# Up's first half ahead for 20 pairs instead of 8, modulation columns asked for by running estimates, and high priority for the latency chains

## The chip, the cores and the metric

The kernel runs on one core of a Trainium2 chip. The metric is the device time in microseconds, median of three runs; below it stands beside the span of one profiled execution of the same program. The engines are TensorE (PE for its matmuls, PEld for its weight loads), VectorE (DVE), ScalarE (ACT), GpSimd (POOL, hardly used) and SyncE (SP), whose queue issues every large transfer.

## The reference, cut to what matters

One decoder layer on 256 tokens of width 2048, in float32:

```
mod = silu(c) @ w_ada + b_ada                    # 6 x 2048: shift, scale, gate, twice
h = rmsnorm(x) * (1 + sc1) + sh1
q_sb,k_sb,v_sb, q_ds,k_ds,v_ds, q_ix,k_ix,w_ix = split(h @ w_in)
o_sb = stick_breaking_attention(q_sb, k_sb, v_sb)   # 8 heads of 128; log-sigmoid, suffix sums, exp
score = sum_h w_ix * relu(rope(q_ix) @ rope(k_ix).T)    # 16 index heads of 64
o_ds = attention(rope(q_ds), rope(k_ds), v_ds) over the 64 best scores of each token   # 8 heads
x = x + g1 * (concat[rmsnorm(o_sb), rmsnorm(o_ds)] @ w_out)
h2 = rmsnorm(x) * (1 + sc2) + sh2
u = h2 @ w_up                                    # 2 x 5504 columns: gate and value
u = conv_b + causal depthwise conv of width 3 over u
x = x + g2 * ((silu(gate) * val) @ w_down)
return rmsnorm(x)
```

## The kernel before, in words

**Weights.** Every weight is read once, in pieces of 128x2048 float32 (1 MB), each by one DMA that SP issues (`load`, L135) into one of four `raw` buffers. A float32 product is made of three products of a narrower type: `split` (L142) takes 1024 columns of a piece, ACT casts them to the high part (L145), DVE subtracts to get the low part (L146), and PE runs high x high, high x low and low x high. In `nat` (L149) the activations are stationary and 512 weight columns move; in `trn` (L171) the weights are stationary and 256 tokens move, in three matmuls; in `fold` (L157) high and low of the tokens stand side by side, so that one matmul of 512 columns and one of 256 do the same.

**Modulation.** The 96 columns of `mod` (128 values each) are independent of all else. One column is either a 1 MB load with one multiply-and-accumulate on DVE (`ada`, L223, tile `wa`), or it belongs to a group of four columns done on PE (`ada_pe`, L194, tiles `wg`, `ap`, `rw`, `aq`): four 1 MB loads with 4 matmuls each, a copy by ACT, four transposes and a short reduction. The list `PEG` names the groups on PE by their first column. Columns wait in two queues (`pending`, `pend_pe`); `pump` (L378), called at fixed places of the program, sends out as many of each as two strings of digits (`PLAN`) say for that call, and `need` sends out what is required at once.

**Order of the work.** A tile scheduler turns the program into one instruction list per engine; a list is executed in order. `order` adds a dependence where one is wanted. The stages, with the stretch that each has in the profile: norm, first half (8 of 16 k tiles) of the projections A, B, V, QK (0 to 168 us); A and B for the second half (to 222); index scores, top-64 and the sparse (DSA) attention, a long chain over DVE, ACT and PE, with the second half of V as other work for PE (to 284); second half of QK, one head per step, and the eight stick-breaking heads `sb_head` (L666, tiles z, u, o) (to 381); the first halves of the output projection O, on the DSA heads; the norm of the stick-breaking heads, `rms_b` with the tiles `rsb` and then `norm_o` (tiles os, osh, osl) (to 404); the rest of O and the first residual (to 475); the second norm and h2 (to 484); Up, 43 pairs of gate and value tiles U with the convolution and silu (to 968); Down, W (to 1207); the last norm.

**Up before.** A pair takes two 1 MB loads, `wU` f,0 (k tiles 0 to 7) and f,1 (k tiles 8 to 15). For the first `G0` = 8 pairs the first halves run ahead into eight PSUM banks, with `trn`; h2 for k = 8 to 15 is made meanwhile, as its modulation columns come; then the second halves follow into the same banks. The other 35 pairs run both halves together with `fold` in two banks.

Of the kernel before, what the change touches and what calls it, by code (L numbers as in the profile page):

```python
# [19 lines left out]
P = 128  # L20
# [23 lines left out]
PEG = [4, 40, 48, 76, 52]  # L44
# [10 lines left out]
def layer(ctx: ExitStack, tc: tile.TileContext, a, out):  # L55
# [52 lines left out]

    def rms_b(sqs_, width, y, name, tag):
# [82 lines left out]
    def ada_pe(j0, q, st={}):  # L194
# [4 lines left out]
        w = load(a["wg"][PEG.index(j0), q], 2048, f"wg{j0}{q}")  # L199
# [23 lines left out]
    def ada(j):  # L223
        w = load(a["wa"][j], 2048, f"wa{j}")
# [69 lines left out]

    def rope(x, t, H, rd, o, name):
# [49 lines left out]

    def put(half, dst, src, scale=1.0):
# [5 lines left out]
        elif scale == 1.0:  # L352
# [5 lines left out]
    credit = [0.0, 0.0]  # L358
# [17 lines left out]
    step = [0]  # L376

    def pump():  # L378
        i = step[0]
        step[0] += 1  # L380
        for c, l in enumerate((pending, pend_pe)):
            if i < len(PLAN[c]):
                n = int(PLAN[c][i])
            else:
                credit[c] += RATE[c]
                n = int(credit[c])
                credit[c] -= n
            for _ in range(min(n, len(l))):
                emit(l)
# [127 lines left out]

    for t in range(NT):
# [27 lines left out]
    for t in range(NT):  # L546
# [27 lines left out]
        V.tensor_tensor(out=sacc[0], in0=sacc[0], in1=sacc[1], op=ALU.add)  # L574
        cur, nxt = sacc
# [27 lines left out]
    for t in range(NT):  # L603
# [29 lines left out]
        for g in range(2):  # L633
# [16 lines left out]

    def norm_o(o, rb_, oh, ol):
        for h in range(0, NH, 4):
# [115 lines left out]
    def h2_make(k):  # L768
# [8 lines left out]
        modulate(h2[k // 4][:, k % 4, 0, :], h2[k // 4][:, k % 4, 1, :], x1T[i][:, j, :], am, r2p if k < 3 else r2, sh,  # L777
# [17 lines left out]

    G0 = 8
    uacc = {}

    def do_U(f, i):

        if i == 0:
            uacc[f] = [bank(f"U{f}{gv}") for gv in range(2)] if f >= G0 else bank(f"U{f}")
        w = load(a["wU"][f, i], 2048, f"wU{f}{i}")
        steps = []
        for gv in range(2):
# [5 lines left out]
            for j in range(8):  # L811
# [23 lines left out]
    for f in range(FT):  # L835
# [4 lines left out]
        pump()  # L840
# [5 lines left out]
        else:  # L846
            u = acc
# [120 lines left out]
```

## Time and profile before

| | us |
|---|---|
| median of three runs (1219.72 to 1223.4) | 1222.13 |
| the profiled execution, its own time | 1222.48 |
| its span, first to last instruction | 1220.7 |
| PE busy (95%) | 1154.4 |
| DVE busy (72%) | 879.5 |
| ACT busy (52%) | 632.2 |
| read from HBM | 300.24 MB, 248 GB/s over the span |

PE is busy for 95% of the span, so the 66 us in which it is not are to be looked for by stage, and beside them what PE does that could be done elsewhere or in fewer matmuls. Busy shares of the other engines are means over stages of different kinds.

### The profile page before, as it was taken

How to read it: one execution, taken by the hardware profiler on the slowest of the kernel's cores; microseconds unless marked ns; L12 is line 12 of the kernel's file. 1: busy time of each engine (PE TensorE's matmuls, PEld its weight loads, DVE VectorE, ACT ScalarE, POOL GpSimd, SP SyncE). 2: the span in 40 equal slices, each digit the busy share in tenths (PEclk: the TensorE clock that was granted, in tenths of full speed). 3: DMA queues.
4: the chain of work that ended last, by engine and by line, in shares of the span. 5: the costliest groups of instructions: out<-in, count | busy, mean ns of one | idle time of the engine just before them, and what ended most of it. 6: DMA issues, size and time to landing. Idle time of an engine off the chain costs nothing.

```text
span 1220.7 us, 17725 instructions
## 1 busy us (share of the span) xinstructions
PE 1154.4 (95%) x7120; PEld 1018.6 (83%) x7120; DVE 879.5 (72%) x1267; ACT 632.2 (52%) x1004; POOL 0.2 (0%) x4
## 2 busy tenths in 40 slices
PE   3699999899999797999999999999999999999996
PEld 2578997668878797999888888888888888888885
DVE  4877787689766698878789787787876745454543
ACT  3356554457465344456565556555655644444441
POOL 0000000000000000000000000000000000000000
PEclk9799999899999898999999999999999999999998
DMA  8988899668788498776568666675665555555541
GB/s 308 391 318 333 330 324 335 256 222 329 260 341 331 141 346 306 246 275 238 177 246 336 241 210 225 222 254 208 246 224 202 178 198 183 196 184 189 191 139 69
DMA packets 43282, 303.48 MB, mean 249 GB/s; under 512 B 4928, under 2 KB 5440, under 8 KB 7232
## 3 DMA queue, kind: packets, MB, share of 16 engines
q1 hardware_dynamic: 43200, 302.35, 68.1%
q8 instruction: 55, 0.90, 0.3%
q14 instruction: 27, 0.22, 0.0%
HBM read 300.24 MB, written 2.10 MB: 248 GB/s over the span
## 4 chain that ended last, share of the span: by engine, by line
PE 89%; DVE 6%; ACT 3%; DMA 1%; issue 1%; SPq 0%; DVEq 0%; ACTq 0%
PE U L168 21%; PE W L168 13%; PE U L166 11%; PE W L166 7%; PE U L173 3%; PE U L174 3%; PE U L175 3%; PE O L174 3%; PE O L175 3%; PE QK L173 3%; PE QK L175 3%; PE O L173 3%; PE QK L174 3%; DVE wa L225 2%; PE ap L202 1%; PE A L151 1%
## 5 line engine op out<-in xcount | busy, mean ns | idle before, releaser
L225 DVE SCALAR_TENSOR_TENSOR wa<-wa,scb 128x2048 f32<-128x2048 f32 x76 | 173.2, 2284 | 3.8 <-DMA wa<-wa 3.5
L844 ACT COPY u<-U 128x256 f32<-128x256 f32 x70 | 26.1, 372 | 116.6 <-PE U L168 116.6
L845 DVE TENSOR_TENSOR u<-U,u 128x256 f32<-128x256 f32 x70 | 29.3, 420 | 58.7 <-ACT u L844 58.7
L855 DVE SCALAR_TENSOR_TENSOR uc<-u,par,uc 128x255 f32<-128x255 f32 (+1 forms) x140 | 63.8, 478 | 0.8
L851 ACT ACTIVATE uc<-u,par 128x256 f32<-128x256 f32 x70 | 41.9, 601 | 0.0
L862 ACT CAST aT<-uc 128x256 fp32r<-128x256 f32 x43 | 17.4, 404 | 33.3 <-DVE uc L861 33.3
L323 ACT ACTIVATE amul<-mod,b,par 128x1 f32<-128x1 f32 x32 | 12.1, 385 | 42.8 <-DVE wa L225 42.6
L890 DVE SCALAR_TENSOR_TENSOR x1T<-W,mod,x1T 128x256 f32<-128x256 f32 x16 | 7.7, 481 | 31.1 <-PE W L166 31.1
L741 ACT ACTIVATE x2q<-x1T 128x256 f32<-128x256 f32 x15 | 6.3, 418 | 39.1 <-DVE x1T L736 39.0
L326 ACT ACTIVATE mod<-mod,par 128x1 f32<-128x1 f32 x32 | 8.5, 294 | 30.5 <-DVE wa L225 29.4
L202 PE MATMUL ap<-wg,csil 128*32 128x512 f32 x160 | 23.5, 642 | 0.7 <-DMA wg<-wg 0.5
L857 ACT ACTIVATE uc<-uc 128x256 f32<-128x256 f32 x43 | 17.9, 416 | 7.7 <-DVE uc L855 7.6
L861 DVE TENSOR_TENSOR uc<-uc 128x256 f32<-128x256 f32 x43 | 18.2, 422 | 2.8
L863 DVE TENSOR_TENSOR aT<-uc,aT 128x256 fp32r<-128x256 f32 x43 | 18.0, 418 | 0.8 <-ACT aT L862 0.7
L855 DVE SCALAR_TENSOR_TENSOR uc<-U,par,uc 128x255 f32<-128x255 f32 (+1 forms) x32 | 15.0, 478 | 1.0 <-ACT uc L851 0.6
L686 ACT ACTIVATE sbt<-sbt 128x384 f32<-128x384 f32 x8 | 4.2, 525 | 20.6 <-DVE sbt L685 20.6
L202 PEld LDWEIGHTS ap<-wg,csil 128*32 128x32 f32 x160 | 4.3, 115 | 9.4 <-issue 7.0
L736 DVE SCALAR_TENSOR_TENSOR x1T<-O,mod,xT 128x256 f32<-128x256 f32 x16 | 7.0, 479 | 6.7 <-PE O L175 6.7
L555 PE MATMUL rel<-ws,qixT 64*128 64x128 f32 (+1 forms) x64 | 9.8, 390 | 1.5 <-ACT rl L560 1.5
L207 ACT COPY rw<-ap 128x512 f32<-128x512 f32 x5 | 2.9, 581 | 15.5 <-PE ap L202 15.5
L283 PE MATMUL cb<-ident,csil 128*128 128x128 f32 x16 | 3.6, 423 | 7.6 <-DMA ident<-ident 7.6
L151 PE MATMUL A<-wA00h,hh 128*128 128x512 f32 x4 | 2.5, 669 | 8.5 <-ACT hh L318 8.5
(2810 smaller groups left out, 4042.8 us busy)
## 6 DMA issues: line engine op xcount, KB each, us to landing
wU<-wU SPq DMA_DIRECT2D x86, 1024.0 KB, 4.8
wa<-wa SPq DMA_DIRECT2D x76, 1024.0 KB, 6.3
wD<-wD SPq DMA_DIRECT2D x43, 1024.0 KB, 4.8
wg<-wg SPq DMA_DIRECT2D x20, 1024.0 KB, 7.1
wA<-wA SPq DMA_DIRECT2D x16, 1024.0 KB, 6.7
wQK<-wQK SPq DMA_DIRECT2D x16, 1024.0 KB, 6.1
wO<-wO SPq DMA_DIRECT2D x16, 1024.0 KB, 5.7
xT<-xT SPq DMA_DIRECT2D x4, 512.0 KB, 6.0
```

The lines of the kernel that those rows point to most:

```text
L166: T.matmul(pt[:, 1, :], lhsT=wl, rhs=x[:, 0, :], start=False, stop=stop)
L168: T.matmul(pt, lhsT=wh, rhs=x, start=first, stop=stop)
L173: T.matmul(pt, lhsT=wh, rhs=xh, start=first, stop=False)
L174: T.matmul(pt, lhsT=wh, rhs=xl, start=False, stop=False)
L175: T.matmul(pt, lhsT=wl, rhs=xh, start=False, stop=last)
L202: T.matmul(pt[32 * j:32 * j + 32, :], lhsT=csil[:, k:k + 1].to_broadcast([P, 32]), rhs=w[:, j * 512:(j + 1) * 512], start=q == 0, stop=q == 3)
L225: i = V.scalar_tensor_tensor(out=w, in0=w, scalar=1.0, in1=scb, op0=ALU.mult, op1=ALU.mult, accum_out=mod[:, j:j + 1])
L844: A.copy(out=u[:, gv, :], in_=acc[gv][:, 1, :])
L845: V.tensor_tensor(out=u[:, gv, :], in0=acc[gv][:, 0, :], in1=u[:, gv, :], op=ALU.add)
L851: A.activation(uc[:, gv, :], u[:, gv, :], AF.Identity, scale=par[:, PCW + 3 * i + 2:PCW + 3 * i + 3], bias=par[:, PCB + i:PCB + i + 1])
L855: V.scalar_tensor_tensor(out=uc[:, gv, sft:S], in0=u[:, gv, 0:S - sft], scalar=par[:, o:o + 1], in1=uc[:, gv, sft:S], op0=ALU.mult, op1=AL ...
L861: V.tensor_tensor(out=uc[:, 1, :], in0=uc[:, 0, :], in1=uc[:, 1, :], op=ALU.mult)
```

## The change

1. Two PE groups fewer: columns 48 to 51, 76 to 79 and 52 to 55 go to DVE, columns 44 to 47 to PE. So there are 12 `wg` loads instead of 20, and 84 `wa` loads instead of 76, as many megabytes in all.
2. `PLAN` and `RATE` go. `pump` is called ahead of every weight load, and sends out columns by three running estimates `clk`: when PE, DVE and the DMA queue would be done with what has been emitted. It sends one (two at most) while the queue's estimate is at least 11.5 us behind PE's: a DVE column if DVE's is at least 6 us behind too, else a PE load. Every helper that emits work adds to the estimates with `spend`.
3. `G0` goes from 8 to 20. Each first half is copied by ACT out of its PSUM bank into an SBUF tile `ut` (128x512 a pair), and added back by DVE after the second half. So 12 more pairs run with `trn` instead of `fold`.
4. `ahead` (a high priority of the scheduler) marks `rms_b`, `rope`, `put`, `sb_head`, `norm_o`, `resid` and the modulation of h2, and `begin`/`end` put the blocks of the index scores, the top-64 and the DSA attention under it.

The diff, cut to its core:

```diff
-PEG = [4, 40, 48, 76, 52]
+PEG = [4, 40, 44]
-PLAN = ("4030000001001101102020110210000...", "0000000000000000000000000000011...")
-RATE = (0.4, 0.7)
+G0 = 20
+    def ahead(f):
+        def g(*args, **kw):
+            with tc.high_priority():
+                return f(*args, **kw)
+        return g
...
+    clk = {"pe": 0.0, "dve": 0.0, "dma": 8.0}
+    def spend(pe=0.0, dve=0.0):
+        clk["pe"] += pe
+        clk["dve"] = max(clk["dve"], clk["pe"] - 10.0) + dve
-    def load(src, n, name):
+    def load(src, n, name, weight=True):
+        if weight:
+            pump()
+        clk["dma"] = max(clk["dma"], clk["pe"] - 14.0) + 3.04 * n / 2048
+        if weight:
+            clk["pe"] = max(clk["pe"], clk["dma"] + 5.0)
+            spend(0.0, 2.45 * n / 2048)
...
     def pump():
-        i = step[0]
-        step[0] += 1
-        for c, l in enumerate((pending, pend_pe)):
...
+        for _ in range(2):
+            if clk["dma"] + 11.5 > clk["pe"]:
+                return
+            if pending and clk["dve"] + 6.0 <= clk["pe"]:
+                emit(pending)
+            elif pend_pe:
+                emit(pend_pe)
+            else:
+                return
...
     def do_U(f, i):
-        if i == 0:
-            uacc[f] = [bank(f"U{f}{gv}") for gv in range(2)] if f >= G0 else bank(f"U{f}")
+        if f < G0:
+            uacc[f] = bank(f"U{f}{i}")
+        elif i == 0:
+            uacc[f] = [bank(f"U{f}{gv}") for gv in range(2)]
...
     for f in range(G0):
         do_U(f, 0)
-        pump()
+        if f % 4 == 0:
+            ut.append(b8([P, 4, 2, S], F32, f"ut{f}"))
+        A.copy(out=ut[-1][:, f % 4, :, :], in_=uacc.pop(f))
...
         else:
-            u = acc
+            u = ut[f // 4][:, f % 4, :, :]
+            V.tensor_tensor(out=u, in0=acc, in1=u, op=ALU.add)
```

**Where instructions stand, first place:** SP's list from the loads of QK's first half on (wQK00 to wQK07 are those weights, wa with a number is that DVE column), in the kernel before:

```order
L137 DMA wQK00_847<-wQK_0 128x2048
L137 DMA wQK01_908<-wQK_0 128x2048
L137 DMA wa9_968<-wa 128x2048
L137 DMA wQK02_972<-wQK_0 128x2048
L137 DMA wa26_1032<-wa 128x2048
L137 DMA wQK03_1036<-wQK_0 128x2048
L137 DMA wQK04_1097<-wQK_0 128x2048
L137 DMA wa10_1157<-wa 128x2048
L137 DMA wa27_1160<-wa 128x2048
L137 DMA wQK05_1164<-wQK_0 128x2048
```

and in the changed kernel:

```order
L164 DMA wQK00_850<-wQK_0 128x2048
L164 DMA wa26_910<-wa 128x2048
L164 DMA wQK01_914<-wQK_0 128x2048
L164 DMA wa10_974<-wa 128x2048
L164 DMA wQK02_978<-wQK_0 128x2048
L164 DMA wa27_1038<-wa 128x2048
L164 DMA wQK03_1042<-wQK_0 128x2048
L164 DMA wa11_1102<-wa 128x2048
L164 DMA wQK04_1106<-wQK_0 128x2048
L164 DMA wa28_1166<-wa 128x2048
```

Weights and columns now alternate strictly here, eight columns for eight weights. The same alternation holds for the loads of the first 20 first halves of Up, 20 `wU` with 16 `wa`.

**Second place:** DVE's list at the end of the stick-breaking heads (rsbv, rsbl, rsby: the norm's small vectors; os, osl: the heads scaled and their low part; wO110l, wO111l: splits for O; sbt, ws: the last head's scores and the sum of squares), before:

```order
L146 TENSOR_TENSOR wO110l<-wO_3554,wO110h 128x1024
L146 TENSOR_TENSOR wO111l<-wO_3554,wO111h 128x1024
L121 TENSOR_SCALAR rsbv<-rsbp 128x2
L225 SCALAR_TENSOR_TENSOR wa_3678,mod<-wa_3678,scb 128x2048
L124 SCALAR_TENSOR_TENSOR rsbl<-rsby 128x2
L125 TENSOR_TENSOR rsbl<-rsbl,rsbv 128x2
L126 SCALAR_TENSOR_TENSOR rsby<-rsbl,rsby 128x2
L654 TENSOR_TENSOR os<-os,rsb 128x1024 x2
L657 TENSOR_TENSOR osl<-os,osh 128x1024 x2
```

and in the changed kernel:

```order
L173 TENSOR_TENSOR wO110l<-wO_3476,wO110h 128x1024
L734 TENSOR_TENSOR sbt<-u_3125,sbt 128x384
L173 TENSOR_TENSOR wO111l<-wO_3476,wO111h 128x1024
L745 TENSOR_TENSOR ws<-ws,sbt 128x256
L135 TENSOR_SCALAR rsbv<-rsbp 128x2
L138 SCALAR_TENSOR_TENSOR rsbl<-rsby 128x2
L139 TENSOR_TENSOR rsbl<-rsbl,rsbv 128x2
L140 SCALAR_TENSOR_TENSOR rsby<-rsbl,rsby 128x2
L697 TENSOR_TENSOR os<-os,rsb 128x1024 x2
L257 SCALAR_TENSOR_TENSOR wa_3739,mod<-wa_3739,scb 128x2048
L700 TENSOR_TENSOR osl<-os,osh 128x1024 x2
```

The modulation column has moved from inside the norm's chain to between os and osl, and the last head's step (sbt, ws) now stands among the last splits. On PE the same place reads, before, the last matmuls of the first halves of O and then the norm:

```order
L173 MATMUL O_3207<-odh,wO301h 128x256
L174 MATMUL O_3207<-odl,wO301h 128x256
L175 MATMUL O_3207<-odh,wO301l 128x256
L115 MATMUL rsbp<-nones,ws 128x1 x2
L129 MATMUL rsbb<-ident,rsby 128x128 x2
L173 MATMUL O_3204<-osh,wO010h 128x256
```

and in the changed kernel the last head (u, o) stands after all but four of them:

```order
L731 MATMUL u_3125<-sbt,cst 128x384
L732 MATMUL u_3125<-sbt,nones 128x128
L205 MATMUL O_3140<-odh,wO301l 128x256
L203 MATMUL O_3140<-odh,wO301h 128x256
L204 MATMUL O_3140<-odl,wO301h 128x256
L205 MATMUL O_3140<-odh,wO301l 128x256
L737 MATMUL o_3130<-sbt,vsb 128x256
L738 MATMUL o_3130<-sbt,vsb 128x128
L129 MATMUL rsbp<-nones,ws 128x1 x2
L143 MATMUL rsbb<-ident,rsby 128x128 x2
```

Before, 117 matmuls of O stand between the last head's o and rsbp; now none does.

**Third place:** DVE's list in the DSA stage (V1000l, V1002l: the first two splits of V's second half; qi1u, qi1v, ki1u: index ropes; qx1, kx1: ropes of q and k; scw, m: index scores and the top-64), before:

```order
L306 TENSOR_TENSOR ws<-ki1u,ki1v 128x16
L304 TENSOR_TENSOR qi1v<-qix,scw 128x16x8
L305 TENSOR_TENSOR qi1v<-qix,scw 128x16x8
L306 TENSOR_TENSOR qix<-qi1u,qi1v 128x16x16
L146 TENSOR_TENSOR V1000l<-V10w_2297,V1000h 128x1024
L146 TENSOR_TENSOR V1002l<-V10w_2297,V1002h 128x1024
L566 SCALAR_TENSOR_TENSOR scw<-rl_1905,wix,cm 128x128
```

and in the changed kernel, where they now stand 50 places behind the first score:

```order
L615 MAX m_1945<-scw 128x8
L337 TENSOR_TENSOR kx1v<-ws,scw 128x16
L334 TENSOR_TENSOR qx1u<-qds,scw 128x256
L338 TENSOR_TENSOR kx1v<-ws,scw 128x16
L616 MATCH_REPLACE scw<-m_1945,scw 128x128
L339 TENSOR_TENSOR ws<-kx1u,kx1v 128x32
L173 TENSOR_TENSOR V1000l<-V10w_2329,V1000h 128x1024
L337 TENSOR_TENSOR qx1v<-qds,scw 128x8x16
```

V's matmuls on PE, which stand between those of the scores before, come only after the DSA queries' transposes now.

## Rows read from the trace of the kernel before

**Rows 1.** The page: busy times of the engines over the span, and one costly group.

```profile
PE 1154.4 (95%) x7120; PEld 1018.6 (83%) x7120; DVE 879.5 (72%) x1267; ACT 632.2 (52%) x1004; POOL 0.2 (0%) x4
L844 ACT COPY u<-U 128x256 f32<-128x256 f32 x70 | 26.1, 372 | 116.6 <-PE U L168 116.6
```

**Rows 2.** Windows by stage: us, busy PE PEld DVE ACT POOL, PEclk, DMA share, GB/s.

```profile
0.00:62.00 62.00, 33.22 (x133) 23.13 (x134) 41.24 (x83) 24.53 (x46) 0.20 (x4) 0.86 0.91 348
62.00:210.00 148.00, 145.51 (x840) 128.03 (x839) 114.77 (x119) 82.02 (x130) 0.00 (x0) 1.00 0.89 332
210.00:284.00 74.00, 68.33 (x378) 48.57 (x371) 59.47 (x161) 37.46 (x91) 0.00 (x0) 0.93 0.68 250
284.00:400.00 116.00, 107.91 (x791) 93.10 (x790) 85.67 (x114) 65.76 (x131) 0.00 (x0) 0.99 0.82 309
400.00:484.00 84.00, 74.31 (x592) 72.99 (x591) 65.62 (x82) 37.19 (x57) 0.00 (x0) 0.93 0.72 266
484.00:1207.00 723.00, 722.62 (x4382) 650.81 (x4383) 506.42 (x700) 383.88 (x549) 0.00 (x0) 1.00 0.60 213
```

**Rows 3.** A window of tile ap alone: PE, PEld, ACT busy, PEclk, DMA share, GB/s.

```profile
284.00:400.00 116.00, 9.98 (x64) 1.82 (x64) 1.15 (x2) 0.99 0.82 309
```

**Rows 4.** Timeline of PE: start, duration, instruction, [idle before, releaser].

```profile
340.03 0.39 PE L175 MATMUL QK<-hh,wQK1600l 128*128 128x256 f32 x1 [0.57 <-DVE wQK1600l L146]
...
375.23 0.66 PE L210 MATMUL aq<-ident,rw 128*128 128x128 f32 x4 [1.21 <-ACT rw L207]
```

**Rows 5.** Timeline of PE in Up, first halves and folded pairs.

```profile
492.36 0.28 PE L173 MATMUL U<-h,wU001h 128*128 128x256 f32 x1
...
494.16 0.28 PE L173 MATMUL U<-h,wU001h 128*128 128x256 f32 x1
...
590.38 1.98 PE L168 MATMUL U<-h,wU900h 128*128 128x512 f32 x8
...
601.49 1.98 PE L168 MATMUL U<-h,wU1000h 128*128 128x512 f32 x8
```

**Rows 6.** Groups of DVE by form (us busy, mean ns), two stretches.

```profile
L855 DVE SCALAR_TENSOR_TENSOR uc<-U,par,uc 128x254 f32<-128x254 f32 x16 | 7.6, 478 | 0.4
L861 DVE TENSOR_TENSOR uc<-uc 128x256 f32<-128x256 f32 x9 | 3.8, 421 | 0.5
L146 DVE TENSOR_TENSOR wU400l<-wU,wU400h 128x1024 fp32r<-128x1024 f32 x1 | 1.2, 1226 | 0.4 <-ACT wU400h L145 0.4
...
L353 DVE TENSOR_TENSOR vsb<-V,vsb 128x512 f32<-128x512 f32 x4 | 2.6, 678 | 0.0
```

**Rows 7.** Timelines of PE and DVE in the DSA stage.

```profile
230.85 1.23 DVE L146 TENSOR_TENSOR V1000l<-V10w,V1000h 128x1024 fp32r<-128x1024 f32 x1 [3.48 <-ACT V1000h L145]
...
232.31 1.61 PE L555 MATMUL rel<-ws,qixT 64*128 64x256 f32 x8 [1.22 <-ACT rl L560]
```

**Rows 8.** Timeline of DVE at the norm of the stick-breaking heads.

```profile
395.72 1.23 DVE L146 TENSOR_TENSOR wO111l<-wO,wO111h 128x1024 fp32r<-128x1024 f32 x1 [1.67 <-ACT wO111h L145]
396.86 0.15 DVE L121 TENSOR_SCALAR rsbv<-rsbp 128x2 f32<-128x2 f32 x1
396.93 2.28 DVE L225 SCALAR_TENSOR_TENSOR wa<-wa,scb 128x2048 f32<-128x2048 f32 x1
...
400.87 2.36 DVE L654 TENSOR_TENSOR os<-os,rsb 128x1024 f32<-128x1024 f32 x2 [1.19 <-ACT rsb L132]
```

**Rows 9.** Timeline of PE at the same place.

```profile
399.74 0.69 PE L129 MATMUL rsbb<-ident,rsby 128*128 128x128 f32 x2 [4.73 <-DVE rsby L126]
...
403.22 0.58 PE L173 MATMUL O<-osh,wO010h 128*128 128x256 f32 x1 [2.80 <-ACT osh L656]
```

**Rows 10.** Windows of 20 us in which loads are dense, columns as in rows 2.

```profile
140.00:160.00 20.00, 20.00 (x169) 20.00 (x169) 16.97 (x21) 11.65 (x24) 0.00 (x0) 1.00 0.87 329
180.00:200.00 20.00, 20.00 (x90) 16.57 (x89) 16.48 (x16) 9.10 (x14) 0.00 (x0) 1.00 0.94 344
360.00:380.00 20.00, 17.21 (x121) 14.49 (x119) 14.02 (x19) 14.35 (x29) 0.00 (x0) 1.00 0.90 368
```

More of the change, by code (lines that the diff above doesn't have):

```diff
@@ L69, in sm, with begin, end @@
         return wp.tile([P, n], F32, name=name, tag="sm", bufs=8)
+    def ahead(f):
[3 more added lines that the diff above has]
+        return g
+    guard = []
+    def begin():
+        guard.append(tc.high_priority())
+        guard[-1].__enter__()
+    def end():
+        guard.pop().__exit__(None, None, None)
     psum_pool = [None]
@@ L107, in rb @@
         return wp.tile([P, S], F32, name=name, tag="rb", bufs=2)
+    @ahead
     def rms_b(sqs_, width, y, name, tag):
@@ L149, in nat @@
     def nat(pt, xh, xl, wh, wl, first, last):
+        spend(3 * (pt.shape[-1] + 32) / 2400)
         T.matmul(pt, lhsT=xh, rhs=wh, start=first, stop=False)
@@ L157, in fold @@
     def fold(steps):
+        spend(0.348 * len(steps))
         lo_first = narrow[0] and not any(s[4] for s in steps)
@@ L171, in trn @@
     def trn(pt, xh, xl, wh, wl, first, last):
+        spend(0.36)
         T.matmul(pt, lhsT=wh, rhs=xh, start=first, stop=False)
@@ L198, in ada_pe @@
         pt = st[j0]
-        w = load(a["wg"][PEG.index(j0), q], 2048, f"wg{j0}{q}")
+        w = load(a["wg"][PEG.index(j0), q], 2048, f"wg{j0}{q}", False)
+        spend(0.85 if q < 3 else 1.4)
         for j in range(4):
@@ L223, in ada @@
     def ada(j):
-        w = load(a["wa"][j], 2048, f"wa{j}")
+        w = load(a["wa"][j], 2048, f"wa{j}", False)
+        spend(0.0, 2.4)
         i = V.scalar_tensor_tensor(out=w, in0=w, scalar=1.0, in1=scb, op0=ALU.mult, op1=ALU.mult,
@@ L293, in layer @@
                            op1=ALU.mult)
+    @ahead
     def rope(x, t, H, rd, o, name):
@@ L310, in modulate @@
         h = s2([P, S], F32, name)
+        spend(0.0, 0.9)
         if not variant:
@@ L344, in layer @@
     qk = [b8([P, 8, S], F32, f"qk{i}") for i in range(2)]
+    @ahead
     def put(half, dst, src, scale=1.0):
@@ L351, in put @@
                 A.mul(out=dst, in_=src, mul=scale)
-        elif scale == 1.0:
+            return
+        spend(0.0, 0.53)
+        if scale == 1.0:
             V.tensor_tensor(out=dst, in0=src, in1=dst, op=ALU.add)
@@ L374, in emit @@
             emitted.update(range(j, j + 4))
-    step = [0]
     def pump():
-        i = step[0]
-        step[0] += 1
-        for c, l in enumerate((pending, pend_pe)):
-            if i < len(PLAN[c]):
-                n = int(PLAN[c][i])
-            else:
[L385 to L389, printed above, removed]
+        for _ in range(2):
[5 more added lines that the diff above has]
+                emit(pend_pe)
+            else:
+                return
     def need(j):
@@ L515, in layer @@
     ptag[0] = "acc"
+    begin()
     for t in range(NT):
@@ L538, in layer @@
     sc_n = [0]
+    end()
     pump()
+    begin()
     def sc_t(L, name):
@@ L574, in layer @@
         V.tensor_tensor(out=sacc[0], in0=sacc[0], in1=sacc[1], op=ALU.add)
+        spend(8.0, 20.0)
         cur, nxt = sacc
@@ L583, in layer @@
         V.tensor_tensor(out=mb[t], in0=mb[t], in1=cmt, op=ALU.add)
+        end()
         pump()
+        begin()
     for t in range(NT):
@@ L642, in layer @@
                 A.activation(od[:, h, t * P:(t + 1) * P], pv[:, j, :], AF.Copy, scale=par[:, PDG + h:PDG + h + 1])
+        spend(10.0, 8.0)
+        end()
         pump()
+        begin()
     for w_ in (4, 2):
@@ L649, in layer @@
     odl = b8([P, NH, S], F32R, "odl")
+    @ahead
     def norm_o(o, rb_, oh, ol):
@@ L657, in norm_o @@
             V.tensor_tensor(out=ol[:, sl, :], in0=o[:, sl, :], in1=oh[:, sl, :].bitcast(F32), op=ALU.subtract)
+            spend(0.0, 2.5)
     norm_o(od, rdb, odh, odl)
+    end()
     pump()
+    begin()
+    end()
     os_ = b8([P, NH, S], F32, "os")
     sbt = b8([P, D], F32, "sbt")
+    @ahead
     def sb_head(h):
+        spend(3.0, 1.6)
         q = qk[h // 4][:, (h % 4) * 2, :]
@@ L732, in layer @@
     sq2 = ws[:, 1536:1792]
+    @ahead
     def resid(dst, acc, gate, res, sqsum, k, name):
+        spend(0.0, 0.9)
         resid_i[0] = V.scalar_tensor_tensor(out=dst, in0=acc, scalar=gate, in1=res, op0=ALU.mult, op1=ALU.add)
@@ L776, in h2_make @@
         sh = mod_cols(k, 64, 48, am, PN2, b2)
-        modulate(h2[k // 4][:, k % 4, 0, :], h2[k // 4][:, k % 4, 1, :], x1T[i][:, j, :], am, r2p if k < 3 else r2, sh,
+        ahead(modulate)(h2[k // 4][:, k % 4, 0, :], h2[k // 4][:, k % 4, 1, :], x1T[i][:, j, :], am, r2p if k < 3 else r2, sh,
                  f"g2_{k}", False)
@@ L817, in do_U @@
                 else:
-                    trn(uacc[f][:, gv, :], x[:, 0, :], x[:, 1, :], wh[:, sl], wl[:, sl], k == 0 and gv == 0,
-                        k == KT - 1 and gv == 1)
+                    trn(uacc[f][:, gv, :], x[:, 0, :], x[:, 1, :], wh[:, sl], wl[:, sl], j == 0 and gv == 0,
+                        j == 7 and gv == 1)
         fold(steps)
@@ L839, in layer @@
         acc = uacc.pop(f)
-        pump()
+        spend(0.0, 3.8 if f >= G0 else 3.5)
         if f >= G0:
```

6 lines of the change are left out of this document (1 added, 5 removed).

## The prediction

> **What bounds the kernel now.** I read the page's busy times first: PE 1154.4 us of 1220.7, DVE 879.5, ACT 632.2 [rows 1]. So PE bounds it on the whole, but the mean hides where it does not. The windows by stage tell that [rows 2]: PE is idle for 62.0 - 33.2 = 28.8 us in the opening, 2.5 us from 62 to 210, 5.7 in the DSA stage (74.0 - 68.3), 8.1 in QK's second half, the heads and the first of O (116.0 - 107.9), 9.7 in the rest of O and the second norm, and 0.4 of 723 us in Up and Down. The granted clock is 0.99 to 1.00 in the long stages, so a matmul taken out there is worth its time at the upper of the two levels. Where PE is idle for nothing (62 to 210, 484 to 1207), only fewer or shorter matmuls help; from 210 to 484 waits count as well. The opening, the two norms' own chains in front of h2 and at the end, and Down keep their instructions and nearly their order, so they are counted at nothing.
>
> **(a) Two groups off PE.** Two of the five groups lie between 284 and 400; their ap matmuls keep PE busy for 9.98 us there, eight loads' worth [rows 3]. Neighbours overlap these by some hundredths at each of the eight places, so I take 9.5. Each group also has four transposes, 0.66 us on the record and about 0.4 in the stream as a third of it overlaps its neighbours, and the last of them waits 1.21 us for ACT's copy [rows 4]: 0.8 + 1.2. In all -11.5. This counts in full if PE stays the bound of that stretch. It was busy for 107.9 of 116 us, DVE for 85.7 and DMA for 0.82 [rows 2], so the other ends would be about -6, if a queue took up half of it. DVE gets eight columns more, 8 x 2.28 us [rows 8] = 18.2 us, and by the loads' order they go beside the first halves of Up, where PE is the bound; there is room for them as Up and Down have 723 - 506 = 217 us of idle DVE [rows 2].
>
> **(b) Twelve more pairs with `trn`.** A folded pair takes 601.49 - 590.38 = 11.11 us of PE [rows 5]. A matmul of `trn` takes (494.16 - 492.36) / 15 = 0.12 us from start to start [rows 5]; a pair has 2 loads x 16 blocks x 3 = 96, so 11.52 us. Twelve pairs: 12 x 0.41 = +4.9. This is on the path, as PE has no idle time there, and it is the surest term.
>
> Beside it stand 20 copies by ACT of 128x512 and 20 additions by DVE. ACT's copy of half that size is 0.37 us [rows 1], so 0.4 to 0.8; ACT is busy for 384 of 723 us in that stretch [rows 2], the copies stand two loads behind the splits in its list, and I count nothing. DVE's second half of an early pair has two splits of 1.23, four convolution steps of 0.48, two products of 0.42 and now one addition of 0.68 (taken from the same shape in V) [rows 6]: 2.45 + 1.91 + 0.84 + 0.68 = 5.88 us by durations, against 48 x 0.12 = 5.76 us of PE for that half. But on DVE the next instruction starts ahead of a split's end: 396.86 - 395.72 = 1.14 us for one of 1.23 [rows 8]. Scaled by that, 5.88 becomes an estimate of 5.45 us, under PE's 5.76, and I count nothing here either. Ends: 0 to +7 (below).
>
> **(c) The DSA stage.** Before, DVE splits V's weights at 230.85, ahead of the scores, and while `rel` waits for ACT's relu (1.22 us once it does) PE has V to do [rows 7]. In the change the scores and ropes go first and V's splits come 50 places later, so V's matmuls are no filler for the scores any more, but the chain of scores and top-64 ends earlier, and the V matmuls fill the later waits for softmax instead. PE's idle time in this stage was 5.7 us [rows 2]; gaining half of it is one end (-3), doubling it the other (+6). Nearest is a small loss, since the filler left is the same matmuls with more waits gathered at the front: +1.
>
> **(d) The end of the heads.** Before, rsbb waits 4.73 us for DVE's rsby, and O 2.80 us for osh [rows 9]: 7.5 us idle. Two things in that chain are no part of the norm: wO111l, which keeps DVE until 396.95, and the column of 2.28 us behind rsbv [rows 8]. The column is gone from there in the change: up to -2.3. But the last head now ends right in front of the norm, where it had 117 matmuls of O (117 x 0.12 = 14 us) behind it: its wait for Exp (o), the sum of squares (ACT then DVE) and the norm have nothing under them. I put two waits of 1.5 us each for these, nearest to the 1.21 and 1.67 us that PE and DVE wait for one ACT step [rows 4, 8], and 1.0 for the addition and the statistics behind them: 4.0 - 2.3 = +1.7. Ends: -2 (the chain is short and the column all that mattered), +3.
>
> **(e) The DMA queue.** In QK's first half and beside Up's first halves, weights and columns alternate: each 5.76 us of PE takes two loads, 2.88 us per load. Where loads were dense 329, 344 and 368 GB/s were moved at DMA shares of 0.87, 0.94 and 0.90 [rows 10]; at a full share these would be 378, 366 and 409, or 2.77, 2.87 and 2.56 us for 1.049 MB. So it just fits, with four buffers as slack: +0.7, ends 0 to +4 while the queue isn't the bound.
>
> The Trainium skill's page "DMA: Bandwidth & Descriptors", section "Bandwidth", gives 341 GB/s for a 1 MB transfer and 425 for 16 MB; by the first a load would take 3.07 us and the queue would bind, by the second 2.47 and it never would. The trace's 368 GB/s over 20 us [rows 10] lies above the first, so the smaller figure is not a ceiling here.
>
> **(f) Small waits.** The first of QK waits 0.57 us for a split [rows 4], and others like it are a us or two in this stretch; with steps marked as going ahead some go and some come: -1.1, ends -2 to +2.
>
> **Sum:** -11.5 + 4.9 + 1.0 + 1.7 + 0.7 - 1.1 = -4.3 us. The profiled execution took 1222.5 us by its own time, so 1218.2; it stood 0.35 us above the median of the runs, so about 1218.0.
>
> **Rivals.** *R1, the DMA queue becomes the bound* in the 24 steps with two loads (8 of QK, 16 of Up). It decides from 2.88 us per load. At the 344 GB/s actually moved [rows 10] a load takes 3.05 us: 24 x 2 x 0.17 = 8; at 329, 3.19 us, 15. With 11.5 in place of (e)'s 0.7: 1229. For it: these windows had PE busy all the time and the queue nearly full. Against: their shares were below 1. *R2, PE starves in the DSA stage*: V's splits are late by so much that (c) is +6, all of its upper end: 1223, no change. For it: the idle time before the scores' matmuls; against: PE had only 5.7 us of idle there, the later waits have V. *R3, DVE bounds the early second halves*: by durations 5.88 us, plus 0.23 of waits for ACT's casts (a wU split waited 0.4 [rows 6]), so 0.35 us over PE's 5.76, 20 times: +7, 1225. Against: the overlap on DVE. *R4, the marked chains give more back*: (c) -3, (d) -2, (f) -2, so 8.6 less: 1209.5. For it: PE has 23.5 us of idle time from 210 to 484 [rows 2], and every one of the waits shown is for an engine that had other work in its list; against: in an in-order list what goes ahead displaces something that feeds PE too.
>
> **How the numbers follow.** About 0.3%, 3.7 us, is what can be told from no change: faster is below 1218.5, slower above 1225.8. Forecast 0.45, with its own range 1213.5 to 1222 from the nearer ends of (c) to (f): 0.26 of it faster, 0.19 within. R1 0.12, all slower. R2 0.14, 0.11 within and 0.03 slower. R3 0.07, 0.03 within, 0.04 slower. R4 0.22, all faster. So faster 0.48, same 0.33, slower 0.19. The range reaches into R4 and R1 on its ends: 1208 to 1228.
>
> **What would show it.** (a): 96 of 160 ap matmuls left, none between 284 and 400, and that stretch, up to the last head, shorter by about 11 us. (b): pairs 8 to 19 at 11.5 us each. (c): idle of PE from the last A to the first head near 6 to 7 us. (d): rsbb's and osh's waits, and new ones before the last o. (e): PE without gaps on DMA in QK's first half and in Up's first 20 halves; gaps of 0.2 us or more at each load there would be R1. R3 would show as waits of Up's matmuls on L146 in the second halves. The forecast is wrong if the heads' stretch isn't shorter (then PE was not its bound), or if a wait on DMA comes up where there was none.

## The result, and the profile after

The changed kernel takes 1230.4 us (median of 4 runs, 1229.8 to 1230.7) against 1220.9 for the kernel before (4 runs too, 1218.2 to 1223.4): a ratio of 1.0077, 95% interval 1.0056 to 1.0097. It is slower by 9.5 us, where 4 us faster was forecast, and it lies above the range of 1208 to 1228. The profiled execution's span is 1228.7 us against 1220.7, and these 8.0 us are what has to be found.

Windows by stage of the changed kernel (columns as in [rows 2], stretch by stretch the counterpart of them):

```profile
0.00:62.00 62.00, 33.13 (x132) 23.00 (x133) 38.11 (x79) 22.84 (x42) 0.20 (x4) 0.86 0.90 337
62.00:210.00 148.00, 143.74 (x824) 125.99 (x823) 116.91 (x121) 81.91 (x132) 0.00 (x0) 1.00 0.91 342
210.00:284.00 74.00, 66.47 (x364) 47.22 (x363) 55.06 (x153) 32.38 (x73) 0.00 (x0) 0.91 0.59 218
284.00:400.00 116.00, 106.48 (x759) 96.98 (x759) 91.87 (x120) 70.10 (x143) 0.00 (x0) 0.96 0.69 244
400.00:484.00 84.00, 76.98 (x609) 76.10 (x608) 65.58 (x89) 37.07 (x58) 0.00 (x0) 0.93 0.70 252
484.00:1207.00 723.00, 716.89 (x4698) 658.96 (x4697) 526.29 (x705) 386.06 (x550) 0.00 (x0) 1.00 0.63 227
```

The new thing is in the last line: PE was idle for 0.4 us of that stretch before, and for 6.1 us now. Where windows shift against each other the starts of the stages say more. PE's timeline, the kernel before, at the start of Up, of pair 20 and of Down:

```profile
484.38 0.55 PE L173 MATMUL U<-h,wU000h 128*128 128x256 f32 x1 [2.73 <-DVE g L312]
...
712.62 1.98 PE L168 MATMUL U<-h,wU2000h 128*128 128x512 f32 x8
...
968.23 1.98 PE L168 MATMUL W<-aT,wD00h 128*128 128x512 f32 x8
```

and the changed kernel, with the start of the second halves (wU010h) as well:

```profile
477.80 0.55 PE L203 MATMUL U<-h,wU000h 128*128 128x256 f32 x1 [2.73 <-ACT h L347]
...
597.29 0.28 PE L203 MATMUL U<-h,wU010h 128*128 128x256 f32 x1
...
712.49 2.00 PE L197 MATMUL U<-h,wU2000h 128*128 128x512 f32 x8
...
975.96 1.98 PE L197 MATMUL W<-aT,wD00h 128*128 128x512 f32 x8
```

Up starts 6.6 us earlier, the 20 pairs cost that lead exactly, and the 23 folded pairs, which nothing in the diff touches, lose 7.9 us. By stage, with the end of A's second half (213.07 before, 214.80 now) as one more mark:

| stretch | forecast, us | measured, us |
|---|---|---|
| start to the end of A | +0.7 (e, a part of it beside Up) | +1.7 |
| end of A to Up: (a), (c), (d), (f) | -9.9 | -8.3 |
| Up, pairs 0 to 19: (b) | +4.9 | +6.5 |
| Up, pairs 20 to 42 | 0 | +7.9 |
| Down and the end | 0 | +0.3 |
| sum | -4.3 | +8.0 |

What the folded pairs wait for is on DVE. Its timeline in the changed kernel beside pair 24 (start, duration, instruction, idle before and releaser):

```profile
756.13 0.42 DVE L899 TENSOR_TENSOR u<-U,u 128x256 f32<-128x256 f32 x1 [0.22 <-ACT u L898]
758.71 2.29 DVE L257 SCALAR_TENSOR_TENSOR wa<-wa,scb 128x2048 f32<-128x2048 f32 x1 [2.16 <-DMA wa<-wa]
760.93 0.08 DVE L257 DVE_READ_ACCUMULATOR wa<-wa,scb 128x1 f32 x1
760.93 0.42 DVE L899 TENSOR_TENSOR u<-U,u 128x256 f32<-128x256 f32 x1
761.27 0.48 DVE L910 SCALAR_TENSOR_TENSOR uc<-u,par,uc 128x255 f32<-128x255 f32 x1
761.66 1.22 DVE L173 TENSOR_TENSOR wU2410l<-wU,wU2410h 128x1024 fp32r<-128x1024 f32 x1
762.79 0.87 DVE L910 SCALAR_TENSOR_TENSOR uc<-u,par,uc 128x254 f32<-128x254 f32 x2
763.58 1.22 DVE L173 TENSOR_TENSOR wU2411l<-wU,wU2411h 128x1024 fp32r<-128x1024 f32 x1
```

The modulation column is next in DVE's list, but its load has not landed; DVE stands for 2.16 us, and the two splits of the pair's second load stand behind it. What PE and DVE waited for in that stretch, 712 to 884 us, the changed kernel (us in total, times, longest):

```profile
PE U L195 <- DVE wU2411l L173: 0.7, 1, 0.7
PE U L195 <- DVE wU3011l L173: 0.7, 1, 0.7
...
DVE wa L257 <- DMA wa<-wa: 21.6, 14, 2.7
```

So it is no lack of engine time: DVE was idle for 21.6 us on 14 landings. PE's own waits, eight of 0.2 to 0.7 us on the second load's splits, make 4.8 us; the other 3 of the 7.9 show no waiter's name, but they stand in the same pairs: 22 to 34 together took 7.9 us more than 11.11 each, and from pair 35 on, where no column is left on DVE, a pair takes 11.11 again. In the load queue 15 columns (81 to 95) stand one to a pair, each between a pair's two weight loads, from pair 21 to pair 35; before, six stood in that stretch, each behind a pair's second load.

Why the column is late stands in three more rows, SP's wait for a free buffer, the issue of the column's load, and ACT's cast for the split that stands behind the column on DVE:

```profile
SPq L164 <- DVE wU2311l L173: 3.4, 1, 3.4
752.64 0.33 SPq L164 DMA_DIRECT2D wa<-wa  x1
756.00 1.05 ACT L172 CAST wU2410h<-wU 128x1024 fp32r<-128x1024 f32 x1
```

SP could issue the load only when wU2311l, a split of the pair before, had freed one of the four `raw` buffers. DVE comes to the column 3.9 us after that issue (at 756.55), and the column is used 6.1 us after it. Pair 24's second load had landed by then, as ACT cast it from 756.00 on; its splits waited for the column alone.

### The profile page after: what moved, and what is told of

Its sections match the earlier page's. It is cut to its first block, busy times and chain, and to the rows that moved or that the text cites. A ratio compares the mean times of both kernels' runs of the same rounds, so it can differ in the third digit from the quotient of the medians.

```text
span 1228.7 us, 18409 instructions
## 1 busy us (share of the span) xinstructions
PE 1153.8 (94%) x7432; PEld 1036.7 (84%) x7432; DVE 900.1 (73%) x1277; ACT 631.7 (51%) x998; POOL 0.2 (0%) x4
## 4 chain that ended last, share of the span: by engine, by line
PE 43%; DVE 14%; DMA 6%; ACT 2%; issue 2%; DVEq 0%; SPq 0%
PE W L197 13%; PE W L195 7%; DMA wa<-wa 6%; PE U L197 5%; DVE uc L910 3%; PE U L204 3%; PE U L205 3%; PE U L203 3%; DVE wa L257 3%; PE U L195 3%; PE O L204 2%; PE O L205 2%; PE O L203 2%; DVE uc L916 1%; ACT aT L917 1%
## 5 line engine op out<-in xcount | busy, mean ns | idle before, releaser
L257 DVE SCALAR_TENSOR_TENSOR wa<-wa,scb 128x2048 f32<-128x2048 f32 x84 | 192.0, 2287 | 33.1 <-DMA wa<-wa 32.8
L898 ACT COPY u<-U 128x256 f32<-128x256 f32 x46 | 17.1, 372 | 50.4 <-PE U L197 50.4
L910 DVE SCALAR_TENSOR_TENSOR uc<-u,par,uc 128x255 f32<-128x255 f32 x92 | 42.0, 477 | 0.3
L906 ACT ACTIVATE uc<-u,par 128x256 f32<-128x256 f32 x46 | 27.6, 601 | 22.9 <-DVE u L899 22.9
L899 DVE TENSOR_TENSOR u<-U,u 128x256 f32<-128x256 f32 x46 | 19.4, 422 | 24.7 <-ACT u L898 24.5
L910 DVE SCALAR_TENSOR_TENSOR uc<-ut,par,uc 128x255 f32<-128x255 f32 (+1 forms) x80 | 33.2, 478 | 0.0
L906 ACT ACTIVATE uc<-ut,par 128x256 f32<-128x256 f32 x40 | 21.8, 593 | 0.1
L902 DVE TENSOR_TENSOR ut<-U,ut 128x512 f32<-128x512 f32 x20 | 13.8, 691 | 6.4 <-PE U L205 6.4
L884 ACT COPY ut<-U 128x512 f32<-128x512 f32 x20 | 11.5, 577 | 3.4 <-PE U L205 3.4
L608 DVE SCALAR_TENSOR_TENSOR scw<-rl,wix,scw 128x128 f32<-128x128 f32 (+1 forms) x28 | 10.2, 413 | 0.8 <-ACT rl L596 0.7
```

What stands on the lines that cost most here:

```text
L257: i = V.scalar_tensor_tensor(out=w, in0=w, scalar=1.0, in1=scb, op0=ALU.mult, op1=ALU.mult, accum_out=mod[:, j:j + 1])
L899: V.tensor_tensor(out=u[:, gv, :], in0=acc[gv][:, 0, :], in1=u[:, gv, :], op=ALU.add)
L906: A.activation(uc[:, gv, :], u[:, gv, :], AF.Identity, scale=par[:, PCW + 3 * i + 2:PCW + 3 * i + 3], bias=par[:, PCB + i:PCB + i + 1])
L910: V.scalar_tensor_tensor(out=uc[:, gv, sft:S], in0=u[:, gv, 0:S - sft], scalar=par[:, o:o + 1], in1=uc[:, gv, sft:S], op0=ALU.mult, op1=AL ...
```

## Experiments

The first four ask which stretch the time went in, and whether place or amount of the columns does it.

**Place of the columns.** The edit keeps the estimates, and asks only ahead of a folded pair's first load:

```diff
-    def load(src, n, name, weight=True):
-        if weight:
+    def load(src, n, name, weight=True, ask=True):
+        if weight and ask:
             pump()
...
-        w = load(a["wU"][f, i], 2048, f"wU{f}{i}")
+        w = load(a["wU"][f, i], 2048, f"wU{f}{i}", ask=f < G0 or i == 0)
```

> The changed kernel, but in the folded pairs of Up columns are asked for only ahead of a pair's first load, not between its two loads; as many columns in the same stretch (15, one a pair). Theory P (place): DVE reaches the column before it has landed and waits 1 to 2 us with the next splits behind it; with the column one load earlier it has landed by then, the folded pairs 20 to 42 take 11.11 us each again instead of 11.46, and the time falls by about 8 us to 1222 to 1223. Rival A (amount): one column of 2.29 us beside a folded pair's own 8.5 us of DVE is simply too much for 11.1 us: the time stays at 1229 to 1231.

Measured: 1223.7 us (1221.9 to 1224.6, 10 runs), 1.0016 of before, interval 1.0006 to 1.0025: 6.8 us less than the changed kernel. The windows 712 to 884 us, the changed kernel first, then this one (columns as in [rows 2]):

```profile
712.00:884.00 172.00, 167.16 (x953) 146.51 (x952) 145.33 (x209) 95.08 (x147) 0.00 (x0) 1.00 0.75 267
```

```profile
712.00:884.00 172.00, 172.00 (x992) 152.39 (x992) 150.65 (x217) 102.06 (x157) 0.00 (x0) 1.00 0.77 274
```

PE has no gap, while DVE is busier than in the changed kernel (150.7 us of 172, against 145.3) with the same 15 columns. The 23 folded pairs take 255.6 us, as in the kernel before; all of the 7.9 us is back there, and pair 20 starts 1.0 us later. In the groups by line over 712 to 900 us the column's idle time is 0.0 us, where it was 21.6; the row below it is the column beside pair 24, issued at 744.62, so that DVE comes to it 5.8 us after its issue:

```profile
L257 DVE SCALAR_TENSOR_TENSOR wa<-wa,scb 128x2048 f32<-128x2048 f32 x15 | 34.3, 2286 | 0.0
750.41 2.29 DVE L257 SCALAR_TENSOR_TENSOR wa<-wa,scb 128x2048 f32<-128x2048 f32 x1
```

Theory P holds; the amount is not the cause.

**No column in the folded pairs.** The same edit, but with no asking at all in the folded pairs (`ask=f < G0`), and in Down:

```diff
-    for j in range(80, 96):
-        need(j)
-    V.tensor_tensor(out=mod[:, 80:96], in0=mod[:, 80:96], in1=par[:, PB + 80:PB + 96], op=ALU.add)
...
-        w = load(a["wD"][:, q * 2048:(q + 1) * 2048], 2048, f"wD{q}")
+        w = load(a["wD"][:, q * 2048:(q + 1) * 2048], 2048, f"wD{q}", ask=q % 2 == 0)
...
+            need(80 + k)
...
+            V.tensor_tensor(out=g, in0=g, in1=par[:, PB + 80 + k:PB + 81 + k], op=ALU.add)
```

> The changed kernel, with no column in the folded pairs at all: the last 15 columns are asked for in Down, one for every second load, each just ahead of the residual that needs it. Theory P and rival A both expect the folded pairs at 11.11 us each and 1222 to 1223, if Down's 239 us don't grow; where they do (a column's landing in DVE's list ahead of Down's splits, 15 times 0.3 to 0.7 us), 1227 to 1233.

Measured: 1223.3 us (10 runs), 1.0017, interval 1.0006 to 1.0029. Down takes 239.7 us from its first matmul to its last, as in the changed kernel, and DVE waits for columns there for 1.8 us in all. Both theories expected this, so the run does not choose between them; it shows that a second place with hardly a wait gives the same time.

**No marking of the DSA blocks.** `begin` and `end` do nothing; the helpers keep their mark.

```diff
     def begin():
-        guard.append(tc.high_priority())
-        guard[-1].__enter__()
+        pass
     def end():
-        guard.pop().__exit__(None, None, None)
+        pass
```

> The changed kernel without the marking of the blocks of index scores, top-64 and DSA attention (begin and end do nothing; the marking of the helpers stays). Theory D: the marking puts V's splits behind scores and ropes, and costs what the stretch from the end of A to the first head got longer, about 7 of its 8 us: 1223 to 1225, with V's matmuls among the scores again. Rival E: the matmuls that were missing there are done later without loss (the heads' stretch got shorter by 16 us where 11.5 were counted), so nothing comes back: 1229 to 1232.

Measured: 1216.8 us (5 runs), 0.9958 of before, interval 0.9941 to 0.9976. That is 13.6 us less than the changed kernel, twice what theory D allowed, and its reason fell too: V's first split comes at 252.9 us here and at 253.1 in the changed kernel, so its place is not what the mark changes. The first head starts at 299.6 instead of 311.9. In the stretch from A's end to Up it takes 249.7 us where the changed kernel takes 263.0, and the rows say how, the changed kernel first:

```profile
214.80:477.80 263.00, 238.93 (x1677) 210.39 (x1677) 201.59 (x344) 136.41 (x266) 0.00 (x0) 0.95 0.68 244
```

```profile
214.20:463.86 249.66, 232.37 (x1678) 206.88 (x1677) 200.95 (x344) 136.14 (x266) 0.00 (x0) 0.97 0.70 257
```

PE is idle for 6.8 us less, and practically the same matmuls keep it busy for 6.6 us less, at a higher mean granted clock (0.97 against 0.95). Where the waits were is shown below, with the two edits in one kernel.

**The opening's order.** Three columns are asked for where they were asked for before.

```diff
+            if (pi, j) == (0, 1):
+                need(18)
+                need(2)
+            if (pi, j) == (0, 3):
+                need(20)
             w = load(a["wA"][k], 2048, f"wA{k}")
```

> The changed kernel, with the columns of the opening asked for as before: 17, 1, 18 and 2 ahead of A's second load, 19, 3 and 20 ahead of its fourth. Theory O: the opening's order alone makes B start 2.8 us later (95.7 instead of 92.9), and as PE is without gaps from there to the second half of A all of it comes back: 1227.6. Rival: the opening is bound by the same number of loads either way, and the time stays at 1230.

Measured: 1229.7 us (4 runs; 1.0062, interval 1.0037 to 1.0087), a median 0.8 us below the changed kernel and a span 1.2 below; B starts at 94.1 instead of 95.7. Theory O gets half at most: B's start moves by 1.6 us of the 2.8, the time by 0.8 to 1.2, and the rest of the opening stays unexplained. A median that near is not apart from no change.

The second four: do the two add up, and what do the parts of the change cost or bring by themselves?

**Both edits together** (the place of the columns, and no marked blocks).

> The two edits that gave time back, together: columns in the folded pairs asked for ahead of a pair's first load, and no marking of the index, top-64 and DSA blocks. If the two losses are separate stretches (theory), they add: 1230.4 - 7 - 13.6 = 1210. Rival: with the first gone the columns come later against the second, and only one of them counts: 1216.

Measured: 1210.7 us (4 runs), 0.9915 of before, interval 0.9896 to 0.9934. They add to the microsecond (1210.0 by the sum). Two separate losses, 6.8 and 13.6 us, had turned a gain of 10 us into a loss of 9.

What marking did is on DVE's timeline. The first rounds of the top-64 of the first 128 tokens (each MAX8 is one of eight rounds), and the mask that ends them (bf16, which the attention's logits need), in the changed kernel:

```profile
245.68 0.29 DVE L615 MAX8 m<-scw 128x8 f32<-128x128 f32 x1
249.40 0.29 DVE L615 MAX8 m<-scw 128x8 f32<-128x128 f32 x1
252.04 0.28 DVE L615 MAX8 m<-scw 128x8 f32<-128x128 f32 x1
254.64 0.28 DVE L615 MAX8 m<-scw 128x8 f32<-128x128 f32 x1
...
262.40 0.20 DVE L620 TENSOR_TENSOR scw<-scw,cm 128x128 bf16<-128x128 bf16 x1
```

and in the kernel with both edits:

```profile
241.57 0.28 DVE L614 MAX8 m<-scw 128x8 f32<-128x128 f32 x1
242.81 0.28 DVE L614 MAX8 m<-scw 128x8 f32<-128x128 f32 x1
244.06 0.28 DVE L614 MAX8 m<-scw 128x8 f32<-128x128 f32 x1
245.30 0.28 DVE L614 MAX8 m<-scw 128x8 f32<-128x128 f32 x1
...
253.37 0.21 DVE L619 TENSOR_TENSOR scw<-scw,cm 128x128 bf16<-128x128 bf16 x1
```

These first rounds come every 2.6 to 3.7 us against one every 1.25: with everything marked alike, more of the second block's sums, of the ropes of q and k, and V's splits too, run between the rounds of the one chain that the logits wait for. The mask comes 9 us later, 4.9 of them between the first round and the mask, and the heads start at 311.9 instead of 300.8. That by itself loses little, as PE has other work meanwhile: 128 matmuls of QK run between A's end and the first head, with both edits 48. But they are then missing between the heads, where the first halves of O take their place (all 192 matmuls of them instead of 86), and the bill comes at the end of the heads, when these have run out. PE's timeline there, the changed kernel:

```profile
386.63 0.70 PE L737 MATMUL o<-sbt,vsb 128*128 128x256 f32 x2 [1.44 <-ACT sbt L735]
...
388.94 0.58 PE L129 MATMUL rsbp<-nones,ws 128*128 128x1 f32 x4 [1.39 <-DVE ws L745]
...
390.69 0.43 PE L143 MATMUL rsbb<-ident,rsby 128*128 128x128 f32 x2 [1.18 <-DVE rsby L140]
...
393.92 0.58 PE L203 MATMUL O<-osh,wO010h 128*128 128x256 f32 x1 [2.80 <-ACT osh L699]
...
397.33 0.58 PE L204 MATMUL O<-osl,wO010h 128*128 128x256 f32 x1 [2.61 <-DVE osl L700]
```

These rows answer to [rows 9]. They are 9.4 us of waits, where the kernel with both edits has one of 0.6, and the granted clock goes with them; the windows 380 to 400 us, the changed kernel, then the one with both edits:

```profile
380.00:390.00 10.00, 6.68 (x48) 5.91 (x46) 6.51 (x9) 6.10 (x14) 0.00 (x0) 1.00 0.74 251
390.00:400.00 10.00, 3.90 (x16) 3.37 (x17) 7.34 (x10) 2.90 (x5) 0.00 (x0) 0.56 0.42 161
```

```profile
380.00:400.00 20.00, 19.38 (x162) 19.17 (x161) 17.48 (x18) 9.74 (x14) 0.00 (x0) 1.00 0.69 245
```

With both edits the heads end 16 us earlier, at 371.5, O's matmuls are left over to fill the norm (rsbp at 372.9, rsbb at 379.6 with O between), and the mean granted clock of the stretch stays 1.00, the upper of the two levels, where it was 0.56 after PE's idle time.

**No marking at all**, the changed kernel with `begin` and `end` doing nothing and `ahead` returning the plain call as well.

```diff
-            with tc.high_priority():
-                return f(*args, **kw)
+            return f(*args, **kw)
```

> The changed kernel with no marking at all: neither the DSA blocks nor the helpers (norm, rope, put, heads, residual, h2). Theory M: the harm is in marking the DSA blocks alone, the helpers' marking is of use or of none: 1216 to 1222. Rival: all marking harms, and without any it is below 1214.

Measured: 1231.3 us (4 runs), 1.0089, interval 1.0068 to 1.0111: outside both expectations. The helpers' marks are worth 14.5 us (1231.3 against 1216.8 with them and without the blocks'). PE's timeline shows the largest wait, the keys' transposes waiting for a rope (3.6 us with the helpers' marks, none in the kernel before):

```profile
253.61 0.45 PE L628 MATMUL kdsp<-ident,ws 128*128 128x128 f32 x1 [8.16 <-DVE ws L337]
```

So marking the helpers gave 14.5 us and marking the blocks took 13.6 back. From A's end to Up this kernel without marks takes 266.4 us, only 4.9 less than the kernel before; as no run has the old plan of columns with three groups, what the running estimates cost or gave there by themselves stays open.

**Five groups on PE**, both edits and the old list.

```diff
-PEG = [4, 40, 44]
+PEG = [4, 40, 48, 76, 52]
```

> The kernel of the two edits together, with the five PE groups of before (4, 40, 48, 76, 52) instead of three. Term (a) of the prediction says that two groups cost 11.5 us of PE between A and Up: A's end to Up's start gets longer by 9 to 11.5 us, and the time is 1219 to 1222. Rival: the heads' chain and not PE sets that stretch, so the groups are covered: 1210 to 1214.

Measured: 1217.6 us (10 runs), 7.0 above the kernel with both edits (0.9977 of before, interval 0.9967 to 0.9986). From A's end to Up it takes 261.3 us instead of 250.4, so the two groups cost 10.8 there; 3.3 us come back at the start of Up, before pair 2, where PE waits 2.7 us for h2's first tiles instead of 5.0. The term stands, the total is smaller.

**G0 = 8**, both edits and eight pairs ahead.

```diff
-G0 = 20
+G0 = 8
```

> The kernel of the two edits together, with G0 = 8 instead of 20. Term (b) alone says 4.9 us less (1205), as 12 pairs are folded again. Theory Q (queue): with the fewer groups the columns of h2's second half come late, 11 of them in a row ahead of the first second half, at about 2.9 us each; PE has no first halves left meanwhile and waits for 12 to 25 us at the end of the first halves: 1218 to 1231. So the 20 pairs ahead would be what pays for the two groups.

Measured: 1230.0 us (4 runs), 1.0092, interval 1.0064 to 1.0120: 19.4 above the kernel with both edits. PE's wait at the start of the second halves, and the window in which PE has nothing else:

```profile
536.97 0.58 PE L202 MATMUL U<-h,wU010h 128*128 128x256 f32 x1 [22.48 <-ACT wU010h L171]
```

```profile
515.00:537.00 22.00, 0.03 (x1) 0.03 (x1) 17.87 (x22) 5.50 (x14) 0.00 (x0) 0.55 0.95 359
```

DMA is busy for 0.95 at 359 GB/s: 11 columns in a row have to land before the second halves. Theory Q holds. The longer run of first halves, 12 pairs at 11.52 us instead of 11.11, costs 4.9 us in matmuls and is what gives the columns taken off PE their time.

The last four: which marks hurt, and the best version.

**Only scores and top-64 marked** (columns' place mended): the blocks from `kx` and `qx` on are unmarked.

```diff
+    end()
     for t in range(NT):
         rope(a2[:, t, 80:80 + HD] ...
...
-        end()
+        pass
         pump()
-        begin()
+        pass
```

> The kernel with columns ahead of a pair's first load, and of the marked blocks only the index scores and top-64 (the DSA attention unmarked). Theory I (interleaving): marking scores and top-64 lets block 1's sums, the ropes and V's splits run between the top-64 rounds of block 0, the first mask comes 10 us later (about 260 us instead of 250 to 253), and the heads start as late as in the changed kernel: 1222 to 1225, as with all blocks marked (1223.7). Rival: marking the attention does it, and this is 1209 to 1213.

Measured: 1223.4 us (10 runs; 1.0024, interval 1.0014 to 1.0034), the first mask at 261.7 us. As with all blocks marked (1223.7).

**Only the attention marked**: the mirror image, with `begin()` ahead of that loop and the earlier pairs taken out.

> The same kernel, but of the marked blocks only the DSA attention (with its ropes and its norm), scores and top-64 unmarked. Theory I: the first mask at 251 to 254 us, 1209 to 1213, as with no block marked (1210.7). Rival: 1222 to 1225.

Measured: 1212.0 us (4 runs; 0.9920, interval 0.9903 to 0.9936), the first mask at 255.1 us. Near to no block marked (1210.7). In the time theory I holds: marking scores and top-64 does nearly all of the harm.

**Ropes marked once**: all blocks marked, columns' place mended, `rope` without `@ahead`.

> Columns ahead of a pair's first load, all blocks marked, but the ropes without a mark of their own inside the marked blocks. Theory I: the order among the marked instructions is the trouble, not the second mark of the ropes; the first mask stays at 258 us or later and the time at 1220 to 1226. Rival: the twice marked ropes push the top-64 back, and without that it is 1209 to 1215.

Measured: 1219.3 us (10 runs; 0.9987, interval 0.9977 to 0.9996), the first mask at 261.9 us. The mask stays late, as theory I says, and yet 4.4 us come back; the time lies just below its expected range, so twice marked ropes are a part of the loss, though not by way of that mask. By what way is open: the heads start at 308.4, 2.3 us earlier than with the twofold mark (310.7). So the late mask is what the traces show of the blocks' harm, but not the whole of it.

**The best version**: both edits and the opening's old order.

> The two edits together (1210.7) and the opening's columns asked for as before (which alone gave 0.8 by the median, 1.2 by the span): 1209 to 1210.5. Rival: what the opening gains is waited for again before the DSA stage: 1210.7.

Measured: 1210.2 us (4 runs, 1209.5 to 1212.0), 0.9909 of before, interval 0.9895 to 0.9924. It beats both kernels, by 10.7 us and 20.2 us; the opening's share (0.4 us of median) can't be told from none.

## Why the prediction was wrong

The span came out 12.3 us above the forecast: 7.9 in the folded pairs, about 1.6 each from A's end to Up and in pairs 0 to 19, 1.0 in the opening and 0.3 at the end (the tenth over is rounding). The failed step is in (a).

**(a) the groups: the term was right, the step beside it failed.** The two groups cost 10.8 us of PE where they stood (11.5 forecast). The step that failed is "by the loads' order they go beside the first halves of Up, where PE is the bound; there is room for them". It was true of 16 columns, and it counted DVE's idle time as room. Fifteen went one to a pair into the folded pairs, and there the question was not how much time DVE had but whether the load had landed when DVE's list came to it. Naming what stands behind a column in DVE's list would have named the next splits. The prediction moved the columns and did not follow them past pair 20, where asking ahead of every load, point 2 of the change, put them between a pair's two loads. Its last sign of being wrong, a wait on DMA where there was none, is what came up, on DVE. Price: 7.9 us, which the mended place gave back in these pairs, 6.8 of it in the time. The sign named for (a), a stretch up to the last head that is 11 us shorter, did not show either: from A's end to the last o it got 5.2 us longer, as work of PE moved ahead of that point, and from there to Up 13.5 shorter.

**(b) `trn` for twelve pairs.** 20 x 5.76 = 115.2 us was expected for the second halves and 597.29 to 712.49 is 115.2. The first halves took 119.5 us, 4.3 over their 115.2; before, eight took 48.8 us, 2.7 over their 46.1. That is the start of Up with its waits for h2's first tiles, and it makes the +6.5 for both out of +4.9: the term itself was right.

**(c) the DSA stage.** +1 was forecast, within -3 to +6, and its sign was PE's idle time from the last A to the first head: 7.5 us (97.1 of which 89.5 busy) against 5.7 before (89.2 and 83.6), so +1.9. The stretch got 7.8 us longer all the same, as 128 matmuls of QK run in it instead of 98. The reason given, V as missing filler, is not what the blocks' marks change: V's splits come as late without them. What they did was to cut up the top-64 chain by instructions marked like it, and the price fell due at the heads' end. The sum from A's end to Up (-8.3 against -9.9) came out near by luck: that stretch takes 266.4 us without marks, 249.7 with the helpers' alone and 263.0 with both, so it holds 16.8 us of gain and 13.3 of loss. The rival R4 saw a gain, of 8.6 us; R2 saw a loss, of 6 by late splits of V, and no rival saw the loss by the blocks' own marks.

**(d) the end of the heads.** 9.4 us of waits for 8.0 (the 7.5 of [rows 9] and 0.5 for osl): +1.4 where +1.7 stood, with the new waits on Exp and the sum of squares (1.44 and 1.39 us) as named.

**(e) the DMA queue, and R1.** Beside the first halves a column stood with nearly every weight, and PE had no gap; the changed kernel's window:

```profile
500.00:600.00 100.00, 100.00 (x836) 100.00 (x835) 79.49 (x79) 52.20 (x74) 0.00 (x0) 1.00 0.92 340
```

It just fits, as worked out from [rows 10]; R1 is out. So is R3, since the second halves ran at PE's pace. The Trainium skill's page "DMA: Bandwidth & Descriptors", section "Bandwidth", gives 341 GB/s for a 1 MB transfer (issued by GpSimd there). The 340 GB/s here were what was asked for and no ceiling, since with G0 = 8 a row of such loads moved 359. The opening, counted at nothing, cost 1.7 us by the end of A; its old order of columns gave 1.2 of span back, which can't be told from none.

## What to carry to other kernels

When work is moved to an engine with idle time, find its new place in that engine's list and ask whether its operands are there by then: an in-order engine that stands at a late load holds back everything behind it, and its busy share (0.84 here) does not show it. Before a load is asked for earlier, see that a buffer is free for it: here the column's load waited 3.4 us for one. Here a priority given to a whole stage let the neighbours of its longest chain in between the chain's steps: mark the short steps that one chain waits for, and leave the chain's neighbours unmarked. And take a compound change apart before judging it: here two mendable losses of 7 and 14 us hid a version that is 0.9% faster than the kernel before.

## What the runs showed of the hardware

In the changed kernel a column's load took 4.9 to 6.6 us from its issue to its use in the folded pairs (issued at 752.64 us, used at 758.71), at a mean DMA share of 0.75: DVE, whose list came to it sooner, waited, though the queue was not full on the mean. And a row of loads with PE idle moved 359 GB/s at a share of 0.95, 378 at a full one, against 340 at 0.92, or 370, with PE busy throughout: near enough that PE's work did not visibly slow the loads.
